# Chunks of the experts' weights: half the rows of one expert in place of a quarter of the rows of two

## The chip, the cores and the metric

The kernel runs on one core of a Trainium2 chip. The metric is the device time of one execution in microseconds (us), the median of three runs. Everything is float32; matrix products run on TensorE (PE in the profile), and 16 DMA engines bring all weights from HBM.

## What is computed

Two transformer blocks on 256 tokens of width 1024. The first has attention and a convolutional feed-forward, the second has attention and a mixture of 32 experts. Only the experts of the second block are touched by the change. Cut to that part, the reference is:

```python
def _hierarchical_moe(h, w_group, w_expert, w_gate, w_up, w_down):
    # top-1 group of 4, then top-2 of its 8 experts; 512 (token, expert) places in all
    ...
    def expert_block(args):
        xb, e = args
        return (jax.nn.silu(xb @ w_gate[e]) * (xb @ w_up[e])) @ w_down[e]
    ...
    contrib = y[dest] * w_sorted[:, None].astype(y.dtype)
    return jnp.zeros((n, d), y.dtype).at[tok_sorted].add(contrib)
```

Each expert has `w_gate` and `w_up` of 1024 x 512 and `w_down` of 512 x 1024, 2 MB each; all 32 experts together have 201 MB, and every one of them is read.

## The kernel before

**Chunks and buffers.** All weights of the program come in chunks of 1 MB (128 partitions x 2048 words), in an order that `plan` writes out. `pump` issues the next chunk's DMA on SP's queue as soon as a buffer is free, `done` counts the uses of a chunk and gives its buffer back, and `give` pumps again. SP's order is thus fixed by the order of the code; a DMA waits for the last reader of its buffer, and for the landing of the DMA eight before it on the same queue (the queue has eight semaphores in rotation).

**Pairs of experts.** The experts are worked off in 16 pairs (pair 0 to pair 15), each expert with up to 64 places. For a pair, expert e = 0 takes columns 0 to 63 of TensorE and expert e = 1 columns 64 to 127: the slice `ps[e * 64:e * 64 + 64, :]` as output puts a product on one half of the array. These products are the rows with `128*64` in the trace, all others take the whole array (`128*128`). `times_x` makes the 16 products of gate or of up (k = 0 to 7, and e = 0, 1 for each k), `down` the 16 of the down matrix (4 rows i, two output halves, two experts).

**A chunk before** (`w_pair`) holds, for both experts of a pair, a quarter of the rows: two runs of 4 KB in each partition. It feeds four products in a row, e = 0, 1, 0, 1, and then its buffer is free. Four chunks make gate, four up, four down; the very last one comes in two pieces.

**What else TensorE does in a pair.** `slots` (rows `bank<-base,hot`, `bank<-wt,hot`) transposes the places of a pair and reads their weights; VectorE (DVE) copies the result out (`ST`, `wslot`, which frees the bank). `gather` (rows `bank<-hot,buf`) collects the tokens of the next two pairs, in four PSUM banks of 8 products each (6 and 2 where the order splits them); it needs `hot`, which VectorE makes in `places`, one instruction for each half of the tokens. `act_T` (rows `bank<-base,act`) transposes the activations, and `combine` (rows `bank<-buf,ST`) adds the former pair's result, 8 products a pair, four for each output half.

**What sets the order.** Only SP's order is the code's own. On all other engines a scheduler orders the instructions at build time, by its own model of when a tile is ready; the engines then run that order as it stands, and wait at semaphores. So the code's `times_x` loop is not one stretch on TensorE: products of `combine`, `slots` and `gather` stand between its products, where the scheduler put them. Where a stretch of `128*64` products ends and a `128*128` product follows, both halves of the array have to be through.

Gate and up of pair 4 and of every even pair after it share their stretch with the first half of a `gather`; those of odd pairs don't.

Of the kernel before, what the change touches and what calls it, by code (L numbers as in the profile page):

```python
# [17 lines left out]
D = 1024  # L18
S = 256
TB = 2  # L20
KT = 8
# [97 lines left out]
class Kernel:  # L119
# [219 lines left out]
    def w_pair(self, src, k, part, pieces=1):  # L339
# [8 lines left out]
                self.nc.sync.dma_start(t[:, :, cs], v[:, :, cs])  # L348
        return load

    def w_tiles(self, src, r0):
        v = src[r0:r0 + 256, :].rearrange("(i p) c -> p i c", p=128)

        def load(t):
            self.nc.sync.dma_start(t.rearrange("p (i c) -> p i c", i=2), v)
        return load
# [52 lines left out]
    def plan(self):  # L409
# [8 lines left out]
        w = a["w_in"][0]  # L418
# [10 lines left out]
        for j in range(16):  # L429
            g = self.fm_units("g", up, j * 256)  # L430
            v = self.fm_units("v", up, 4096 + j * 256)
            if j:
                d += self.row_units("d", dn, j * 256 - 256)
            while len(mods) < min(2 * len(VEC), j // 3 + max(0, j - 1)):
                n, part = VEC[len(mods) // 2], len(mods) % 2
# [9 lines left out]
        w = a["w_in_2"][0]  # L445
# [12 lines left out]
        for pr in range(16):  # L458
            for n, w, k in (("gate", a["w_gate_2"][0], KT), ("up", a["w_up_2"][0], KT), ("down", a["w_down_2"][0], 4)):
                for part in range(4):  # L460
                    load = self.w_pair(w[2 * pr:2 * pr + 2], k, part, 2 if (pr, n, part) == (15, "down", 3) else 1)
                    self.experts[n, pr, part] = self.add_raw(n, load)


    def constants(self):
# [995 lines left out]
    def moe(self):  # L1461
# [12 lines left out]
        xt = self.buf(QK_A, [128, KT, 256])  # L1474
# [22 lines left out]
        where = {pr: (i % 2, j * 128) for i, g in enumerate(groups) for j, pr in enumerate(g)}  # L1497
# [63 lines left out]
        def times_x(pr, n, b):  # L1561
            ps = self.bank(b)
            for k in range(KT):
                c = self.experts[n, pr, k // 2]
                for e in range(2):
                    c0 = e * D + (k % 2) * 512
                    self.mm(ps[e * 64:e * 64 + 64, :], xt[:, k, where[pr][1] + e * 64:where[pr][1] + e * 64 + 64], c.tile[:, c0:c0 + 512],
                            k == 0, k == KT - 1)
                if k % 2:
                    self.done(c)  # L1570
            return ps

# [16 lines left out]
        def down(pr, aT, banks):  # L1589
            ps = [self.bank(b) for b in banks]  # L1590
            for i in range(4):
                c = self.experts["down", pr, i]
                for hf in range(2):
                    for e in range(2):
                        c0 = e * D + hf * 512
                        self.mm(ps[hf][e * 64:e * 64 + 64, :], aT[i // 2][:, i % 2, e * 64:e * 64 + 64],
                                c.tile[:, c0:c0 + 512], i == 0, i == 3)
                self.done(c)
            self.weighted(ps[0], W[pr], gate, 0, y[0])
            return ps[1]  # L1600

# [21 lines left out]
        for what in 'a2 q1 a4 b1 r0 a1 b1 r1 a1 b1 s0 b1 h0 b2 b1 h1 b1 s1'.split():  # L1623
            n = int(what[1])
# [19 lines left out]
        for pr in range(16):  # L1644
            banks, others = ((4, 5), (6, 7))[::1 if pr % 2 == 0 else -1]
            if pr < 15:
                g = times_x(pr, "gate", banks[0])
# [3 lines left out]
            if pr < 15:  # L1651
                u = times_x(pr, "up", banks[1])
# [7 lines left out]
            if pr == 15:  # L1660
                assert self.next_dma == len(self.chunks)
                self.rest_of_experts(xn, A, B, gate, acc, self.free[:3])
                gfin = self.buf(self.free[3], [128, D])
                fin = self.buf(self.free[4], [128, TB, D])
                nc.sync.dma_start(gfin, bass.AP(tensor=a["g_final_2"].tensor, offset=a["g_final_2"].offset,
                                                ap=[[0, 128], [1, D]]))
                g, u = times_x(pr, "gate", banks[0]), times_x(pr, "up", banks[1])
# [83 lines left out]
```

## Time and profile before

| | us |
|---|---|
| median of 3 runs (lowest, highest) | 1072.98 (1071.98, 1074.51) |
| the profiled execution, its own time | 1071.89 |
| its span, first to last instruction | 1070.1 |
| busy: PE | 1011.2 |
| busy: DVE | 511.5 |
| busy: ACT | 406.3 |

The page cuts the span in 40 slices of 26.75 us. The experts' stage begins near 600 us. TensorE is busy in nine tenths or more of almost every slice of the program, and from slice 24 on the DMA engines are too. A matmul of float32 leaves two records in the trace: 16 records of `128*64` products are 8 matmuls, 4 on each half of the array. In a row of the timeline an idle time of the engine stands in brackets, with what ended it.

### The profile page before, as it was taken

Reading aid. Unit: us, or ns where it says so; the run is one execution under the profiler, and the core shown is the slowest. Engines: PE = TensorE matmul, PEld = TensorE weight load, DVE = VectorE, ACT = ScalarE, POOL = GpSimd, SP = SyncE. Lnnn points to the kernel's source line nnn. Section 1 sums busy time; section 2 is a strip of 40 time slices with the busy share of each in tenths; the row PEclk is TensorE's granted clock in tenths of the full one; section 3 lists DMA queues with packets and bytes.
Section 4 is the critical chain, followed back from the end, with each engine's and each line's share of the span. In section 5 each row is a group of like instructions: output and inputs, shape, how many; then the busy total and the mean of one; then the engine's idle time right before and its main releaser. Section 6 shows DMA issues by size and latency. Waiting matters only on the chain. (4 is left out here: it accounts for less than half of the span.)

```text
span 1070.1 us, 14717 instructions
## 1 busy us (share of the span) xinstructions
PE 1011.2 (94%) x5927; PEld 695.7 (65%) x5927; DVE 511.5 (48%) x938; ACT 406.3 (38%) x749; POOL 47.7 (4%) x48
## 2 busy tenths in 40 slices
PE   6999999999999999899999999999999999999986
PEld 6887799999999998699867544443343434333332
DVE  5568588978878866648596311121111111111112
ACT  5566556555455555446664120212020202011112
POOL 2001200000000000200043000000000000000000
PEclk9999999999999999899999799999999999999998
DMA  7964654867576767654555499999999999999994
GB/s 200 374 219 128 235 181 164 309 212 257 203 245 224 268 244 253 200 197 142 192 181 200 169 409 409 409 409 408 409 409 409 409 409 409 409 409 409 409 409 180
DMA packets 131520, 313.52 MB, mean 293 GB/s; under 512 B 7229, under 2 KB 59226, under 8 KB 131450
## 3 DMA queue, kind: packets, MB, share of 16 engines
q1 hardware_dynamic: 131082, 312.02, 78.4%
q0 software_dynamic: 368, 0.54, 0.3%
q8 instruction: 47, 0.77, 0.3%
q14 instruction: 23, 0.19, 0.0%
HBM read 311.89 MB, written 1.05 MB: 292 GB/s over the span
## 5 line engine op out<-in xcount | busy, mean ns | idle before, releaser
L210 PE MATMUL bank<-buf,buf 128*128 128x256 f32 (+4 forms) x4152 | 707.2, 382 | 7.1 <-issue 1.8
L210 PEld LDWEIGHTS bank<-buf,buf 128*128 128x128 f32 (+1 forms) x4152 | 494.8, 177 | 177.1 <-issue 127.0
L185 DVE TENSOR_TENSOR buf<-buf,buf 128x1024 fp32r<-128x1024 f32 x150 | 183.3, 1223 | 72.0 <-ACT buf L183 71.3
L183 ACT ACTIVATE buf<-buf 128x1024 fp32r<-128x1024 f32 x154 | 162.3, 1055 | 111.9 <-PE bank L210 101.4
L210 PE MATMUL bank<-buf,aT 128*64 128x512 f32 x512 | 114.8, 595 | 3.3 <-ACT aT L1586 3.3
L1576 DVE TENSOR_TENSOR act<-act,bank 128x512 f32<-128x512 f32 x16 | 11.0, 687 | 210.2 <-PE bank L210 210.2
L1457 DVE SCALAR_TENSOR_TENSOR tmp<-bank,wslot,gffn 128x512 f32<-128x512 f32 x32 | 24.0, 751 | 133.0 <-PE bank L210 131.3
L210 PEld LDWEIGHTS bank<-buf,aT 128*64 128x64 f32 x512 | 37.1, 137 | 69.3 <-issue 60.2
L1575 ACT ACTIVATE act<-bank 128x512 f32<-128x512 f32 x16 | 9.6, 597 | 137.2 <-PE bank L210 137.2
L1458 ACT ACTIVATE buf<-tmp 128x512 fp32r<-128x512 f32 x32 | 20.2, 631 | 107.5 <-DVE tmp L1457 107.5
L947 ACT ACTIVATE buf<-bank,convT 128x256 f32<-128x256 f32 x64 | 36.0, 563 | 53.7 <-PE bank L210 43.6
L1521 ACT ACTIVATE buf<-bank,mod,g_ffn 128x256 f32<-128x256 f32 (+1 forms) x72 | 34.6, 537 | 48.7 <-PE bank L210 48.7
L1586 ACT ACTIVATE aT<-bank 128x256 f32<-128x256 f32 x32 | 10.6, 382 | 95.1 <-PE bank L213 95.1
L210 PE MATMUL bank<-buf,ST 128*128 128x512 f32 x128 | 38.2, 420 | 8.0 <-ACT buf L1458 7.9
L210 PEld LDWEIGHTS bank<-buf,ST 128*128 128x128 f32 x128 | 21.5, 188 | 36.8 <-ACT buf L1458 18.5
L210 PEld LDWEIGHTS bank<-hot,buf 128*128 128x128 f32 x256 | 32.1, 189 | 17.1 <-issue 8.9
L1030 DVE SCALAR_TENSOR_TENSOR bank<-buf,c,bank 128x512 f32<-128x512 f32 x56 | 42.0, 750 | 1.4 <-DMA buf<-in_w_ada_dram 1.1
L210 PE MATMUL bank<-hot,buf 128*128 128x256 f32 (+1 forms) x256 | 36.7, 290 | 3.6 <-ACT act L1575 3.6
L949 DVE SCALAR_TENSOR_TENSOR buf<-bank,convT,buf 128x255 f32<-128x255 f32 x64 | 30.6, 479 | 10.3 <-ACT buf L947 9.9
L951 DVE SCALAR_TENSOR_TENSOR buf<-bank,convT,buf 128x254 f32<-128x254 f32 x64 | 30.7, 480 | 1.3
L210 PEld LDWEIGHTS bank<-diag,buf 128*128 128x128 f32 x112 | 22.1, 272 | 8.7 <-DVE diag L770 4.6
L210 PE MATMUL bank<-diag,buf 128*128 128x128 f32 x112 | 23.7, 363 | 4.2 <-DVE diag L770 2.7
(202 smaller groups left out, 661.7 us busy)
## 6 DMA issues: line engine op xcount, KB each, us to landing
buf<-in_w_up_dram SPq DMA_DIRECT2D x96, 1024.0 KB, 18.2
buf<-in_w_down_dram SPq DMA_DIRECT2D x79, 1024.0 KB, 18.2
buf<-in_w_gate_dram SPq DMA_DIRECT2D x64, 1024.0 KB, 18.3
buf<-in_w_ada_dram SPq DMA_DIRECT2D x24, 1024.0 KB, 5.2
buf<-in_w_in_dram SPq DMA_DIRECT2D x18, 1024.0 KB, 9.7
buf<-in_w_out_dram SPq DMA_DIRECT2D x8, 1024.0 KB, 17.1
buf<-in_w_in_dram SPq DMA_DIRECT2D x6, 512.0 KB, 7.6
buf<-in_x_dram SPq DMA_DIRECT2D x2, 512.0 KB
```

The costliest lines, as they stand in the source:

```text
L183: pin(nc.scalar.activation(H, raw, AF.Copy))
L185: pin(engine.tensor_tensor(L, raw, H, op=ALU.subtract))
L210: return self.nc.tensor.matmul(out, lhsT, rhs, start=start, stop=stop, skip_group_check=True)
L947: nc.scalar.activation(c[:, s, :], u[:, s, :], AF.Identity, scale=cT[:, 128 + n:129 + n], bias=cT[:, 192 + n:193 + n])
L949: nc.vector.scalar_tensor_tensor(c[:, s, 1:], u[:, s, 0:255], cT[:, 64 + n:65 + n], c[:, s, 1:], op0=ALU.mult, op1=ALU.add)
L951: nc.vector.scalar_tensor_tensor(c[:, s, 2:], u[:, s, 0:254], cT[:, n:n + 1], c[:, s, 2:], op0=ALU.mult, op1=ALU.add)
L1030: nc.vector.scalar_tensor_tensor(p.pa, w, s, p.pa, op0=ALU.mult, op1=ALU.add)
L1457: nc.vector.scalar_tensor_tensor(tmp[:n], ps, w, gate[:n, cs], op0=ALU.mult, op1=ALU.mult)
L1458: nc.scalar.activation(y[:, 0], tmp[:n], AF.Copy)
L1521: nc.scalar.activation(xt[:, k, :n], g, AF.Identity, scale=A[:, k:k + 1], bias=B[:, k:k + 1])
L1576: nc.vector.tensor_tensor(act, act, u, op=ALU.mult)
L1586: nc.scalar.activation(aT[i], pt[:, 2 * i:2 * i + 2, :], AF.Copy)
```

## The change

For all chunks but the down chunks of the last pair, a chunk is now half of the rows of one expert's matrix: one run of 8 KB in each partition (`w_half`). The order of the four chunks of a matrix is: expert 0 first half, expert 1 first half, expert 0 second half, expert 1 second half. Each chunk is still 1 MB, their number and the bytes stay, and each is used by four products of gate or up (k = 0 to 3, or 4 to 7, of one expert), or four of down. In the code `times_x` and `down` name the chunk of each product through the table `self.experts`, and `done` is counted for each product in `times_x`.

```diff
+    def w_half(self, src, k, half):
+        n = src.shape[1] * k // 2
+        v = src.rearrange("(p k) c -> p (k c)", k=k)[:, half * n:half * n + n]
+        def load(t):
+            self.nc.sync.dma_start(t, v)
         return load
...
                 for part in range(4):
-                    load = self.w_pair(w[2 * pr:2 * pr + 2], k, part, 2 if (pr, n, part) == (15, "down", 3) else 1)
-                    self.experts[n, pr, part] = self.add_raw(n, load)
+                    if (pr, n) == (15, "down"):
+                        c = self.add_raw(n, self.w_pair(w[2 * pr:2 * pr + 2], k, part, 2 if part == 3 else 1))
+                        c.left = 2
+                        for e in range(2):
+                            self.experts[n, 2 * pr + e, part] = c, e * D
+                    else:
+                        e, half = part % 2, part // 2
+                        c = self.add_raw(n, self.w_half(w[2 * pr + e], k, half))
+                        c.left = k // 2
+                        for i in range(k // 2):
+                            self.experts[n, 2 * pr + e, k // 2 * half + i] = c, i * 2048 // (k // 2)
...
             for k in range(KT):
-                c = self.experts[n, pr, k // 2]
                 for e in range(2):
-                    c0 = e * D + (k % 2) * 512
-                    self.mm(ps[e * 64:e * 64 + 64, :], xt[:, k, ...], c.tile[:, c0:c0 + 512],
-                            k == 0, k == KT - 1)
-                if k % 2:
+                    c, c0 = self.experts[n, 2 * pr + e, k]
+                    self.mm(ps[e * 64:e * 64 + 64, :], xt[:, k, ...], c.tile[:, c0:c0 + 512], k == 0, k == KT - 1)
                     self.done(c)
...
             for i in range(4):
-                c = self.experts["down", pr, i]
                 for hf in range(2):
                     for e in range(2):
-                        c0 = e * D + hf * 512
+                        c, c0 = self.experts["down", 2 * pr + e, i]
+                        c0 += hf * 512
                         self.mm(ps[hf][e * 64:e * 64 + 64, :], aT[i // 2][:, i % 2, e * 64:e * 64 + 64],
                                 c.tile[:, c0:c0 + 512], i == 0, i == 3)
-                self.done(c)
+                for e in range(2):
+                    self.done(self.experts["down", 2 * pr + e, i][0])
```

In the loop over k the code still names the products in the same order. The scheduler does not keep it. On TensorE, where gate of pair 6 begins (`bank_6544` is gate's bank, `bank_6609` that of `slots`, 5607 to 5610 are `combine`, `bank_6663` the first bank of `gather`), the order before is:

```order
L213 MATMUL bank_6609<-base,hot 128x128 x2
L210 MATMUL bank_6609<-wt,hot 128x2 x2
L210 MATMUL bank_6544<-buf_6314,buf_5567 64x512 x4
L210 MATMUL bank_5607<-buf_5566,ST 128x512
L210 MATMUL bank_5609<-buf_5566,ST 128x512
L210 MATMUL bank_5608<-buf_5566,ST 128x512 x2
L210 MATMUL bank_5610<-buf_5566,ST 128x512 x2
L210 MATMUL bank_6544<-buf_6320,buf_5567 64x512 x4
L210 MATMUL bank_6663<-hot,buf_5560 128x256 x2
```

and after the change:

```order
L213 MATMUL bank_6609<-base,hot 128x128 x2
L210 MATMUL bank_6609<-wt,hot 128x2
L210 MATMUL bank_6544<-buf_6314,buf_5567 64x512
L210 MATMUL bank_5607<-buf_5566,ST 128x512
L210 MATMUL bank_5609<-buf_5566,ST 128x512
L210 MATMUL bank_5608<-buf_5566,ST 128x512 x2
L210 MATMUL bank_5610<-buf_5566,ST 128x512 x2
L210 MATMUL bank_6609<-wt,hot 128x2
L210 MATMUL bank_6663<-hot,buf_5560 128x256 x2
L210 MATMUL bank_6544<-buf_6323,buf_5567 64x512
L210 MATMUL bank_6544<-buf_6314,buf_5567 64x512
```

Before, the four products of one chunk stood together; now the one product of expert 0 (from `buf_6314`) stands alone, its partner of expert 1 (from `buf_6323`) comes after `combine`, the second product of `slots` and two of `gather`.

Further on in TensorE's order, where gate of pair 6 ends and up (`bank_6577`) begins, before:

```order
L210 MATMUL bank_6544<-buf_6406,buf_5567 64x512 x4
L210 MATMUL bank_6630<-hot,buf_5560 128x256 x2
L210 MATMUL bank_6630<-hot,buf_5561 128x256 x2
L210 MATMUL bank_6630<-hot,buf_5560 128x256 x2
L210 MATMUL bank_6577<-buf_6412,buf_5567 64x512 x4
```

and after, from gate's last two products on:

```order
L210 MATMUL bank_6544<-buf_6326,buf_5567 64x512
L210 MATMUL bank_6544<-buf_6410,buf_5567 64x512
L210 MATMUL bank_6577<-buf_6412,buf_5567 64x512
L210 MATMUL bank_6630<-hot,buf_5560 128x256 x2
L210 MATMUL bank_6630<-hot,buf_5561 128x256 x2
L210 MATMUL bank_6630<-hot,buf_5560 128x256 x2
L210 MATMUL bank_6630<-hot,buf_5561 128x256 x2
L210 MATMUL bank_6577<-buf_6422,buf_5567 64x512
```

Here too expert 0's first product of up has moved ahead of the `gather` products, away from its partner (from `buf_6422`).

On VectorE, in the same stretch of pair 6 (two `hot` instructions of `places`, the copies out of `slots`' bank, then the product of the activations), before:

```order
L1459 TENSOR_TENSOR buf_5566<-tmp,buf_5566 128x512
L1527 TENSOR_TENSOR hot<-base,rk 128x256
L1459 TENSOR_TENSOR buf_5566<-tmp,buf_5566 128x512
L1527 TENSOR_TENSOR hot<-base,rk 128x256
L1555 CAST ST<-bank_6609 128x256
L1558 COPY wslot<-bank_6609 64x1 x2
```

and after (line numbers have grown by 18):

```order
L1477 TENSOR_TENSOR buf_5566<-tmp,buf_5566 128x512
L1545 TENSOR_TENSOR hot<-base,rk 128x256
L1477 TENSOR_TENSOR buf_5566<-tmp,buf_5566 128x512
L1573 CAST ST<-bank_6609 128x256
L1576 COPY wslot<-bank_6609 64x1 x2
L1545 TENSOR_TENSOR hot<-base,rk 128x256
```

The second `hot` has moved behind the copies.

## Rows read from the trace of the kernel before

**Rows 1.** The page: the span, and the GB/s of its 40 slices.

```profile
span 1070.1 us, 14717 instructions
GB/s 200 374 219 128 235 181 164 309 212 257 203 245 224 268 244 253 200 197 142 192 181 200 169 409 409 409 409 408 409 409 409 409 409 409 409 409 409 409 409 180
```

**Rows 2.** What the matmuls of PE waited for, 640 to 1034 us (us in total, times, longest).

```profile
PE bank L213 <- DVE act L1576: 9.5, 11, 0.9
PE bank L210 <- ACT buf L1458: 7.2, 11, 0.7
...
PE bank L210 <- PE bank L213: 0.2, 1, 0.2
```

**Rows 3.** Timeline of DVE (start, us): the activations' product of pairs 6 and 8.

```profile
785.35 0.69 DVE L1576 TENSOR_TENSOR act<-act,bank 128x512 f32<-128x512 f32 x1 [15.29 <-PE bank L210]
...
843.95 0.69 DVE L1576 TENSOR_TENSOR act<-act,bank 128x512 f32<-128x512 f32 x1 [15.28 <-PE bank L210]
```

**Rows 4.** DMA, 960 to 1000 us: GB/s in 40 slices, and the packets.

```profile
GB/s 418 406 410 401 422 410 406 406 418 406 410 401 422 406 410 401 414 397 406 414 406 414 406 410 414 410 406 414 406 414 406 414 410 410 410 406 410 414 410 410
DMA packets 4246, 16.37 MB, mean 409 GB/s; under 512 B 252, under 2 KB 252, under 8 KB 4245
```

**Rows 5.** The chunks' tiles, 700 to 1040 us: from a DMA's issue to its landing.

```profile
DMA to landing us min/median/max: 18.2/19.0/21.6
```

**Rows 6.** Timeline of SP and of PE: pair 14's gate, issue and first use.

```profile
974.22 12.03 SPq L348 DMA_DIRECT2D buf<-in_w_gate_dram  x4
...
1000.23 1.94 PE L210 MATMUL bank<-buf,buf 128*64 128x512 f32 x8
```

**Rows 7.** Timeline of PE: gate and up of pair 6.

```profile
765.41 0.51 PE L210 MATMUL bank<-wt,hot 128*128 128x2 f32 x4
765.85 1.94 PE L210 MATMUL bank<-buf,buf 128*64 128x512 f32 x8
767.72 1.65 PE L210 MATMUL bank<-buf,ST 128*128 128x512 f32 x6
769.29 1.94 PE L210 MATMUL bank<-buf,buf 128*64 128x512 f32 x8
...
772.30 3.65 PE L210 MATMUL bank<-buf,buf 128*64 128x512 f32 x16
776.65 0.98 PE L210 MATMUL bank<-hot,buf 128*128 128x256 f32 x6 [0.70 <-ACT act L1575]
...
779.86 5.37 PE L210 MATMUL bank<-buf,buf 128*64 128x512 f32 x24
786.09 0.75 PE L213 MATMUL bank<-base,act 128*128 128x128 f32 x4 [0.86 <-DVE act L1576]
```

**Rows 8.** Timeline of PE: down of pair 1 to gate of pair 3.

```profile
646.02 0.61 PE L210 MATMUL bank<-buf,buf 128*64 128x512 f32 x1 [0.23 <-PE bank L213]
646.27 0.64 PE L210 MATMUL bank<-buf,aT 128*64 128x512 f32 x1
...
653.62 7.18 PE L210 MATMUL bank<-buf,buf 128*64 128x512 f32 x31
...
661.85 7.08 PE L210 MATMUL bank<-buf,buf 128*64 128x512 f32 x30
...
674.88 7.09 PE L210 MATMUL bank<-buf,aT 128*64 128x512 f32 x32
681.80 7.04 PE L210 MATMUL bank<-buf,buf 128*64 128x512 f32 x32
```

**Rows 9.** Timeline of DVE in the stretch of rows 7.

```profile
766.68 0.42 DVE L1527 TENSOR_TENSOR hot<-base,rk 128x256 fp32r<-128x256 f32 x1
769.40 0.42 DVE L1555 CAST ST<-bank 128x256 fp32r<-128x256 f32 x1 [2.31 <-PE bank L210]
769.74 0.32 DVE L1558 COPY wslot<-bank 64x1 f32<-64x1 f32 x2
```

**Rows 10.** Timeline of PE: the first `gather` products after gate in pair 4.

```profile
717.12 0.98 PE L210 MATMUL bank<-hot,buf 128*128 128x256 f32 x6 [0.16 <-ACT act L1575]
```

More of the change, by code (lines that the diff above doesn't have):

```diff
@@ L349, in w_pair @@
         return load
+    def w_half(self, src, k, half):
[3 more added lines that the diff above has]
+            self.nc.sync.dma_start(t, v)
+        return load
     def w_tiles(self, src, r0):
@@ L1563, in times_x @@
             for k in range(KT):
-                c = self.experts[n, pr, k // 2]
                 for e in range(2):
-                    c0 = e * D + (k % 2) * 512
-                    self.mm(ps[e * 64:e * 64 + 64, :], xt[:, k, where[pr][1] + e * 64:where[pr][1] + e * 64 + 64], c.tile[:, c0:c0 + 512],
-                            k == 0, k == KT - 1)
-                if k % 2:
+                    c, c0 = self.experts[n, 2 * pr + e, k]
+                    self.mm(ps[e * 64:e * 64 + 64, :], xt[:, k, where[pr][1] + e * 64:where[pr][1] + e * 64 + 64], c.tile[:, c0:c0 + 512], k == 0, k == KT - 1)
                     self.done(c)
```

## The prediction, made blind

> **What bounds the kernel now.** The change touches only the experts' stage, from about 600 us on. I first read the page's slices: the DMA engines move a flat 409 GB/s in the 16 slices from slice 24 on [rows 1]. A flat line is a full queue, so the first question is whether TensorE waits for the weights. The view of waits says no: among what matmuls waited for between 640 and 1034 us there are DVE, ACT and PE itself, five rows in all, and no DMA [rows 2]. The longest of these waits are the hand-overs within a pair, 0.9 us for the activations' product and 0.7 us for the weighted result. The timeline says the same in another way: the same step of pairs 6 and 8 is 843.95 - 785.35 = 58.6 us apart [rows 3], 29.3 us a pair. The queue needs more than that: a pair is 12 chunks of 1.0486 MB, 12.58 MB / 409 GB/s = 30.8 us [rows 4]. Both can hold only because the stage starts with a stock of landed chunks that TensorE eats up. How much of it is left near the end: pair 14's gate chunks are issued from 974.22 us on and first used at 1000.23 us [rows 6]; a chunk lands at most 21.6 us after its issue [rows 5], so at 995.8 us, and 4.4 us are left. TensorE's order of work sets the end, DMA is 4 us behind it, and anything that lengthens TensorE's stage counts in full.
>
> **The change part by part: the transfers.** The 188 chunks in the new shape have the same bytes and the same place in SP's queue; SP issues as many instructions. The packets now are nearly all 4 KB or less (16.37 MB / 4246 = 3.9 KB, [rows 4]); no row shows an 8 KB run. Bounds for its speed: from no gain to the best short slices, 422 GB/s against 409 [rows 4]. Either way it is worth nothing while TensorE is behind the stock; I take nothing. The Trainium skill's page "DMA: Bandwidth & Descriptors" (section on why small descriptors are slow) puts a fixed 3 cycles on each packet of 32-byte beats; by it, as an estimate, 128 + 3 beats twice against 256 + 3 once is 1.1% less time, and its ceiling of 435 GB/s would leave 425 GB/s for 4 KB runs, where the rows have 409. If DMA set the end, the sum by that rule would be about 5 us lower.
>
> **The chunk's two users.** Expert 1's first half is needed right behind expert 0's, not one chunk (four products, 1.8 us) later, and expert 0's buffer comes back some four products later. Price: 1.8 us of the 4.4 us that are left at pair 14, none of it on the path; behind a late chunk TensorE would wait with everything queued on it. If TensorE gets slower, the stock grows and this is covered further.
>
> **TensorE's order.** This is the part that costs. The unit: 24 records of half-array products last 5.37 us, 16 last 3.65 us [rows 7]; 8 records are 4 products, two on each half, so one product takes (5.37 - 3.65) / 2 = 0.86 us and two of different experts run side by side in it. A stretch between two full-array products therefore lasts as many units as its fuller half has products. The trace has one case with a half product set apart. Up of pair 2 had its first expert-0 product pulled ahead of `combine`. The rest, 30 records, lasts 7.08 us, no less than 32 records with 7.04 us [rows 8]: the missing product saves nothing. And the stretch that had it in front lasts 653.62 + 7.18 - 646.02 = 14.78 us against 681.80 + 7.04 - 674.88 = 13.96 us for one without [rows 8]: 0.82 us more. So a product set apart from its partner costs one unit of 0.82 to 0.86 us.
>
> Now the two orders, stretch by stretch. Before, gate and up of a pair are cut at whole chunks (4, 4, 8, 4 and 12 products in pair 6), 16 units in every pair. After, pair 6 has 1, 7, 1, 8 and 15 products, which is 1 + 4 + 1 + 4 + 8 = 18 units. Pairs 4, 8, 10 and 12 are cut alike, and pair 14 into 1, 16, 7, 1 and 7, 18 units too. Pairs 5, 7, 9, 11 and 13 have 1 and 31 products, 17 units. That is 6 x 2 + 5 x 1 = 17 units more, 17 x 0.86 = 14.6 us. Pairs 0 to 3 and 15 keep their stretches; the number of stretches and thus of changes between half and full array stays the same in all.
>
> **A new wait.** In pairs 6, 8, 10 and 12 two `gather` products now follow `combine` and the second `slots` product directly. Their bank is that of `slots`, which DVE frees, and their second operand is the `hot` that moved behind these copies. In the rows DVE begins the cast 769.40 - 769.29 = 0.11 us after `combine` ends, ends the two copies at 769.74 + 0.32 = 770.06, and `hot` takes 0.42 us more [rows 9]: ready 1.2 us after `combine`. TensorE has one `slots` product to do meanwhile, half of 765.85 - 765.41 = 0.44 us [rows 7]. So it waits 1.0 us, with all products of gate queued behind; before, four products (769.29, [rows 7]) covered this. Four such waits are 4.0 us. In pairs 4 and 14 one or sixteen products stand in between and cover it, and in odd pairs nothing asks for the bank. Bounds: none of it (if copies and cast run earlier than I read) to 1.2 us each, 0 to 4.8 us.
>
> The wait for ACT between gate and the first `gather` products of gate's bank, 0.70 us [rows 7], stays: up's first product moved into it runs beside the last of gate, not behind it. In pair 4 it was 0.16 us [rows 10], since other `gather` products stood there; I add 0.5 us. The wait of 0.86 us ahead of the transposes [rows 7] and that for the weighted result stay.
>
> In `down` the order of experts turns from 0, 1, 0, 1 to 0, 0, 1, 1 at one or two places in pairs 4 to 13. I take it as free: at 646.27 us an expert-1 product of down starts 0.25 us after the set-apart expert-0 product, although another expert-0 product stands between the two in the order and cannot have started [rows 8]. Expert 1's half does not wait for expert 0's. If it did, it would cost one unit in each of ten pairs, 8.6 us.
>
> **The sum.** 14.6 + 4.0 + 0.5 = 19.1 us on the path; against the profiled execution's own 1071.89 us that is 1091.0 us. The median of the runs lies 1.1 us above that execution, so I forecast 1092 us, 1.8% slower. Own range: units at 0.82 us and no new wait give 1072.98 + 13.9 = 1087 us; waits of 1.2 us and 0.1 us for each second `slots` product apart give 1072.98 + 20.9 = 1094 us.
>
> **The rivals.** First, faster: the queue sets the end after all, and longer runs speed it up. For it: the queue is full over 16 slices of 26.75 us, 428 us [rows 1]. Against: no matmul waits for it [rows 2], and 4.4 us are in hand. At 422 GB/s the 428 us would shrink by 428 x 13 / 422 = 13.2 us, to 1060 us. It decides only if TensorE's own stage does not grow.
>
> Second, no change: a product set apart is free, because the half it leaves empty is filled by what comes next, and DVE has freed the bank early. Then 1073 us. Against: the 0.82 us measured in rows 8. With the four waits alone it would be 1077 us.
>
> Third, slower by more: the 0, 0, 1, 1 order in `down` costs a unit in each of ten pairs. For it: within one half the order is kept. Against: 646.27 us in rows 8. 1092 + 8.6 = 1101 us.
>
> Fourth, the hand-over: buffers that come back later and chunks needed earlier empty the stock, and the pair takes the queue's 30.8 us instead of 29.3 us in the last third, five pairs, less the 4.4 us in hand: 5 x 1.5 - 4.4 = 3 us, 1076 us. Against: a TensorE that needs about 31.2 us a pair never catches up with the queue.
>
> **How the numbers follow.** Forecast 0.74 (1087 to 1094), third rival 0.10 (up to 1101), no change 0.06, waits alone or hand-over 0.05, faster 0.05. A measurement of this kernel tells apart about 0.2%, or 2.1 us: faster 0.05, same 0.06, slower 0.89. For 8 in 10 the range has to reach from the forecast's lower end, with some room for a unit or a wait that is hidden, to the third rival: 1085 to 1101 us.
>
> **What would show it.** Right: the same step of pairs 6 and 8 some 62.2 us apart (58.6 + 3 x 0.86 + 1.0); single records of half products ahead of `combine`, with the next row a unit later; a bracket of about 1.0 us with DVE as releaser at two `gather` products in pairs 6, 8, 10 and 12; SP waiting for PE, and GB/s in the stage at about 12.58 MB / 31.1 us = 404 instead of a flat 409; down still 7.1 us for 32 records. Wrong: matmuls that wait for a DMA, the step still 58.6 us apart although the order moved, or down at 7.9 us.

## The result: 1.4% slower, and the profile after

| | before | after |
|---|---|---|
| median of the runs on one chip, us | 1072.80 (4 runs, 1071.98 to 1074.51) | 1087.82 (4 runs, 1085.99 to 1088.87) |
| the profiled execution, its own time | 1071.89 | 1088.87 |
| its span | 1070.1 | 1087.1 |

The ratio is 1.0136, with a 95% interval of 1.0117 to 1.0155: 15.0 us by the medians. The two profiled executions are 17.0 us apart.

The page after, span and GB/s of the 40 slices (27.2 us each), beside [rows 1]:

```profile
span 1087.1 us, 14713 instructions
GB/s 202 377 233 133 194 175 214 251 235 268 235 230 217 287 186 262 198 189 130 263 153 119 289 419 420 420 420 419 420 420 419 420 420 421 419 420 420 419 160 39
```

The queue is as full as before, at 420 GB/s in place of 409, and it is through earlier: slice 39 begins at 1032.7 us and is filled for 160 / 420 of it, so the weights are in at about 1043 us by this estimate; the trace has the last chunk's landing at 1044.2 us. Before, slice 40 began at 1043.3 us and was filled for 180 / 409: about 1055 us (the last landing is at 1055.1 us). TensorE ends 17 us later, the queue 11 us earlier.

DMA after, 960 to 1000 us, beside [rows 4]:

```profile
DMA packets 2304, 16.80 MB, mean 420 GB/s; under 512 B 255, under 2 KB 255, under 8 KB 255
```

and the chunks' tiles, 700 to 1040 us, from a DMA's issue to its landing, beside [rows 5]:

```profile
DMA to landing us min/median/max: 8.5/16.0/21.3
```

Nearly all packets are 8 KB now. A chunk lands after 8.5 us at best, where it was 18.2 us, though the rate rose by 2.7% only. That fits fewer transfers standing in the queue: more of the buffers hold chunks that have landed.

What the matmuls waited for after the change, 640 to 1034 us (us in total, times, longest), beside [rows 2]:

```profile
PE bank L213 <- DVE act L1591: 8.5, 10, 0.9
PE bank L210 <- ACT buf L1476: 6.5, 10, 0.7
PE bank L210 <- ACT act L1590: 4.1, 6, 0.7
PE bank L210 <- DVE wslot L1576: 3.4, 4, 0.8
```

The two rows left out are ACT's `aT`, 2.8 us, and PE itself, 0.2 us. Still no DMA. One line is new: four waits for DVE's copy `wslot`, 3.4 us.

DVE after, the activations' product of pairs 6, 7 and 8 (start, us), beside [rows 3]:

```profile
791.63 0.69 DVE L1591 TENSOR_TENSOR act<-act,bank 128x512 f32<-128x512 f32 x1 [18.43 <-PE bank L210]
820.56 0.69 DVE L1591 TENSOR_TENSOR act<-act,bank 128x512 f32<-128x512 f32 x1 [13.29 <-PE bank L210]
853.68 0.69 DVE L1591 TENSOR_TENSOR act<-act,bank 128x512 f32<-128x512 f32 x1 [18.44 <-PE bank L210]
```

Pairs 6 and 8 are 853.68 - 791.63 = 62.05 us apart, against 58.6 us in [rows 3].

TensorE after, gate and up of pair 6, beside [rows 7] (start, duration, instruction, number of records; in brackets the idle time and what ended it):

```profile
769.26 1.07 PE L210 MATMUL bank<-buf,buf 128*64 128x512 f32 x2
770.27 1.66 PE L210 MATMUL bank<-buf,ST 128*128 128x512 f32 x6
771.76 0.28 PE L210 MATMUL bank<-wt,hot 128*128 128x2 f32 x2
772.88 0.47 PE L210 MATMUL bank<-hot,buf 128*128 128x256 f32 x2 [0.84 <-DVE wslot L1576]
773.28 3.65 PE L210 MATMUL bank<-buf,buf 128*64 128x512 f32 x14
776.86 0.74 PE L210 MATMUL bank<-hot,buf 128*128 128x256 f32 x4
777.53 1.07 PE L210 MATMUL bank<-buf,buf 128*64 128x512 f32 x2
778.53 0.50 PE L210 MATMUL bank<-hot,buf 128*128 128x256 f32 x2
778.96 3.65 PE L210 MATMUL bank<-buf,buf 128*64 128x512 f32 x16
783.30 1.21 PE L210 MATMUL bank<-hot,buf 128*128 128x256 f32 x8 [0.68 <-ACT act L1590]
784.44 7.08 PE L210 MATMUL bank<-buf,buf 128*64 128x512 f32 x30
```

In pair 5 (an odd pair; no `gather` among its products):

```profile
741.76 1.07 PE L210 MATMUL bank<-buf,buf 128*64 128x512 f32 x2
742.76 1.66 PE L210 MATMUL bank<-buf,ST 128*128 128x512 f32 x6
744.26 0.28 PE L210 MATMUL bank<-wt,hot 128*128 128x2 f32 x2
744.47 13.95 PE L210 MATMUL bank<-buf,buf 128*64 128x512 f32 x62
```

In pair 6 two stretches hold one product (2 records) each, and each takes 1.00 us until the next row starts. Pair 5 has one such stretch. The 14 records at 773.28 us take 3.65 us, as long as the 16 at 778.96 us: the partner that has gone ahead leaves its place empty.

The step from one pair's activations' product to the next pair's (differences of starts in the same DVE timeline; the rows of pairs 7 and 8 after the change stand above) splits the loss. Start to end of the first four pairs (0 to 3) differs by less than 0.1 us.

| pair | before | after | difference |
|---|---|---|---|
| 4 | 29.67 | 31.66 | +1.99 |
| 5, 7, 9, 11, 13 | 28.16 to 28.17 | 28.92 to 28.93 | +0.76 each, 3.8 |
| 6, 8, 10, 12 | 30.43 to 30.44 | 33.11 to 33.12 | +2.68 each, 10.7 |
| 14 | 30.17 | 31.78 | +1.61 |
| 15 | 30.77 | 28.78 | -1.99 |
| from there to the end | 19.86 | 19.86 | 0 |

The sum is +16.1 us. The other 0.9 us between the two spans lies ahead of pair 0's product (614.4 and 615.3 us), in code that the change doesn't touch; over the profiled executions of this text that point lies between 612.6 and 616.1 us.

Pair 15 is the only pair that got faster. TensorE there before the change:

```profile
1034.19 3.65 PE L210 MATMUL bank<-buf,buf 128*64 128x512 f32 x16 [0.56 <-PEq L1356]
1039.62 10.52 PE L210 MATMUL bank<-buf,buf 128*64 128x512 f32 x48 [1.77 <-issue]
1050.07 0.44 PE L213 MATMUL bank<-base,hot 128*128 128x128 f32 x2
```

and after:

```profile
1053.18 13.95 PE L210 MATMUL bank<-buf,buf 128*64 128x512 f32 x64 [0.57 <-PEq L1374]
1067.06 0.44 PE L213 MATMUL bank<-base,hot 128*128 128x128 f32 x2
```

Ahead of pair 15's products each engine takes a branch (`rest_of_experts`). Before, TensorE did eight products behind it, stood still for 1.77 us, with nothing that it waited for in the profile ("issue"), and went on. After, 64 records run through. Before, the queue was full at this time; after, the last chunk had landed 8 us ahead of TensorE's branch.

### The profile page after: what moved, and what is told of

Read it like the earlier page. It is cut to its first block, busy times and chain, and to the rows that moved or that the text cites. A ratio compares the mean times of both kernels' runs of the same rounds, so it can differ in the third digit from the quotient of the medians.

```text
span 1087.1 us, 14713 instructions
## 1 busy us (share of the span) xinstructions
PE 1026.1 (94%) x5927; PEld 705.8 (65%) x5927; DVE 512.3 (47%) x938; ACT 406.8 (37%) x749; POOL 48.0 (4%) x48
## 3 DMA queue, kind: packets, MB, share of 16 engines
HBM read 311.89 MB, written 1.05 MB: 288 GB/s over the span
## 5 line engine op out<-in xcount | busy, mean ns | idle before, releaser
L210 PE MATMUL bank<-buf,buf 128*128 128x256 f32 (+4 forms) x4152 | 720.7, 381 | 7.8 <-DVE buf L284 2.6
L210 PEld LDWEIGHTS bank<-buf,aT 128*64 128x64 f32 x512 | 40.7, 137 | 66.2 <-issue 58.2
## 6 DMA issues: line engine op xcount, KB each, us to landing
buf<-in_w_gate_dram SPq DMA_DIRECT2D x64, 1024.0 KB, 16.1
```

Of the source, the lines that this page charges most:

```text
L210: return self.nc.tensor.matmul(out, lhsT, rhs, start=start, stop=stop, skip_group_check=True)
```

## The experiments

In all of them TensorE's units are counted as in the prediction: 495 in the program before the change, 512 after. Steps are those of the table above. Each ratio is against the kernel before the change, run on the same chip.

### Does the order cost the time, or the chunk?

The changed kernel with its chunks, but expert 1's product named ahead of expert 0's. Expert 1's chunk lands second, so that no product is ready without its partner, and the scheduler leaves the two together: 495 units.

```diff
             for k in range(KT):
-                for e in range(2):
+                for e in (1, 0):
                     c, c0 = self.experts[n, 2 * pr + e, k]
```

> The changed kernel, all new chunks and their order of transfer kept, but gate and up name expert 1's product ahead of expert 0's for each row k. In the order that results no product stands apart from its partner: gate and up are again 16 units a pair (495 units in the whole program, as before the change; the changed kernel has 512), and there are 20 stretches of half-array products fewer (57 in place of 77). Two `gather` products still follow `combine` directly, but the second `hot` stands ahead of the copies again. Theory of the order (the loss is TensorE's units and the waits they bring): all of it comes back; against 1072.8 us before the change some 20 changes between half and full array go too, about 0.1 us each, so 1069 to 1073 us. Theory of the chunks (the loss is in the new chunks themselves: what they hold, when they are needed and released, the order of experts in `down`): it stays at 1085 to 1088 us. Apart from that: pair 15's 1.8 us of standing still behind the branch, gone after the change, should be back here if it hangs on weights that still come in while TensorE takes the branch (1.8 us within the 1069 to 1073), and stay away if it hangs on the new chunks.

1073.19 us, ratio 1.0012 (0.9995 to 1.0029). The loss is gone but for a rest, with every new chunk in place: it was the order, not what the chunks hold. By the steps 2.2 us of the 16.1 us stay, less than the 4.2 us of the waits named next: pair 4 takes 31.58 us, 1.9 us more than before the change, pairs 6, 8, 10 and 12 take 0.25 to 0.37 us more, odd pairs 0.16 us less. The 2 us that 20 changes between half and full array fewer were to give back don't show in the sum. One expectation failed: five `gather` products wait 0.84 us for `wslot` although the second `hot` stands ahead of the copies. TensorE and DVE in that kernel, pair 6:

```profile
767.75 1.77 PE L210 MATMUL bank<-buf,ST 128*128 128x512 f32 x6
769.56 0.42 DVE L1573 CAST ST<-bank 128x256 fp32r<-128x256 f32 x1 [0.49 <-PE bank L210]
769.90 0.32 DVE L1576 COPY wslot<-bank 64x1 f32<-64x1 f32 x2
770.37 1.17 PE L210 MATMUL bank<-hot,buf 128*128 128x256 f32 x8 [0.84 <-DVE wslot L1576]
```

The cast starts when `combine` ends, 1.7 us after the last `slots` product. And pair 15's standing still is back; in the view of waits, 640 to 1050 us:

```profile
PE bank L210 <- issue: 1.6, 1, 1.6
```

### The half changes

Gate and up in the old chunks, `down` in the new:

```diff
+                    elif n != "down":
+                        c = self.add_raw(n, self.w_pair(w[2 * pr:2 * pr + 2], k, part))
+                        c.left = 4
+                        for e in range(2):
+                            for i in range(2):
+                                self.experts[n, 2 * pr + e, 2 * part + i] = c, e * D + i * 512
                     else:
                         e, half = part % 2, part // 2
```

> Gate and up as before the change (a quarter of the rows of both experts), only `down` in the new chunks. TensorE's order has 16 units a pair as before (495); `down` has the order 0, 0, 1, 1 at two places in each of pairs 4 to 13; the second product of `slots` stands behind `combine`, with four products ahead of the next `gather`. Prediction's theory (0, 0, 1, 1 is free, and four products cover the copies): 1071 to 1074 us, `down` 7.1 us for 32 records. Third rival (each pair loses a unit of 0.86 us in `down`): 8.6 us more, 1081 us, `down` 7.9 us.

1071.37 us, ratio 0.9999 (0.9983 to 1.0015). Two of its `down` rows (pairs 4 and 5):

```profile
730.45 7.26 PE L210 MATMUL bank<-buf,aT 128*64 128x512 f32 x32
757.24 7.14 PE L210 MATMUL bank<-buf,aT 128*64 128x512 f32 x32 [0.47 <-ACT aT L1607]
```

With 0, 0, 1, 1 at two places, 32 records take 7.14 to 7.27 us against 7.09 us before, not 7.9 us. Expert 1's half doesn't wait for expert 0's.

Gate and up in the new chunks, `down` in the old:

```diff
-                    if (pr, n) == (15, "down"):
-                        c = self.add_raw(n, self.w_pair(w[2 * pr:2 * pr + 2], k, part, 2 if part == 3 else 1))
+                    if n == "down":
+                        c = self.add_raw(n, self.w_pair(w[2 * pr:2 * pr + 2], k, part, 2 if (pr, part) == (15, 3) else 1))
```

> `down` as before the change, only gate and up in the new chunks. TensorE has the same 512 units as the changed kernel, with the same products set apart; but `slots` is whole again ahead of `combine`, and on DVE the second `hot` stands ahead of the copies, so that the copies run beside `combine` and the `gather` products behind it find their bank free. Theory of the order, units and wait apart: the four waits of 0.84 us go, 3.4 us of the changed kernel's 1087.8, so 1084 to 1085 us, and no `gather` product waits for DVE. If the waits were only a place where time shows that is lost elsewhere, it stays at 1087 to 1088 us.

1088.08 us, ratio 1.0152 (1.0107 to 1.0198). The whole loss is in gate and up. The expectation failed all the same: the four waits of 0.84 us stay, although `slots` is whole and `hot` out of the way. TensorE and DVE, pair 6:

```profile
768.95 1.65 PE L210 MATMUL bank<-buf,ST 128*128 128x512 f32 x6
770.63 0.42 DVE L1573 CAST ST<-bank 128x256 fp32r<-128x256 f32 x1 [1.44 <-PE bank L210]
770.97 0.32 DVE L1576 COPY wslot<-bank 64x1 f32<-64x1 f32 x2
771.43 0.47 PE L210 MATMUL bank<-hot,buf 128*128 128x256 f32 x2 [0.84 <-DVE wslot L1576]
```

Again the cast waits until `combine` ends. My reason for the wait fell here: it isn't the second `slots` product or `hot`. What cast and `combine` share is `ST`, a single buffer that `combine` reads and the cast overwrites. [rows 9] has the same cast 0.11 us behind `combine`, with 2.31 us of idle time in front of it; only, before, four products stood between `combine` and the `gather` that needed the bank.

Up and `down` in the new chunks, gate in the old (in the diff of the first half change `n == "gate"` in place of `n != "down"`): only up's first product stands apart, in six pairs.

> Gate as before the change, up and `down` in the new chunks. Now only up's first product of expert 0 stands apart, in each even pair from 4 to 14: 501 units, six more than before the change, and no `gather` directly behind `combine`. Theory of the units: 6 x 0.85 = 5.1 us over the kernel before the change, 1076.5 to 1078 us, all of it in the even pairs and nothing in the odd ones; pair 15's 1.7 us behind the branch stay (weights still come in). If a product apart costs less in this place, since it runs beside the last product of gate, a pair's step shows it: below 0.5 us in an even pair, 1072 to 1075 us.

1076.09 us, ratio 1.0048 (1.0031 to 1.0066). Pairs 6, 8, 10 and 12 take 31.19 to 31.22 us, +0.75 to 0.79; pair 4 +0.80, pair 14 +0.83; odd pairs -0.05. Six units cost 4.7 us, 0.79 us each, beside the last product of gate as elsewhere.

### The buffer of `ST`

The kernel with expert 1 named first, and `ST` in two buffers by turns:

```diff
-            st = self.t([128, TB, 128], "ST", F32R, tag="dist")
+            st = self.t([128, TB, 128], "ST", F32R, tag=("dist", "convT")[pr % 2])
```

> The kernel with expert 1 named first (1073.2 us), with one more edit: the copy `ST` of `slots` alternates between two buffers in place of one. TensorE's order is the same, instruction by instruction. In that kernel's trace `gather` waits 0.84 us for DVE in five pairs, and each time DVE's cast begins 0.1 us behind the last product of `combine`. Theory of the one buffer (the cast overwrites the `ST` that `combine` reads, and so can't begin before `combine` is through): the five waits go, 4.2 us, 1069.0 us, below the kernel before the change (1071.7 to 1072.8). Theory of the bank (the cast is late because DVE or `slots` is late): the waits stay, 1073 us. Pair 15's 1.6 us behind the branch stay in either case.

1071.01 us, ratio 0.9989 (0.9979 to 0.9998). TensorE and DVE, pair 6:

```profile
767.34 1.77 PE L210 MATMUL bank<-buf,ST 128*128 128x512 f32 x6
768.24 0.41 DVE L1573 CAST ST<-bank 128x256 fp32r<-128x256 f32 x1
769.04 1.18 PE L210 MATMUL bank<-hot,buf 128*128 128x256 f32 x8
```

The cast runs beside `combine`, and `gather` waits no more: the one buffer is shown as the cause. In time it gave less than the 4.2 us of the five waits. The even pairs from 4 to 12 became 0.8 to 1.0 us faster, four of the five odd pairs (5, 7, 9 and 13) 0.33 to 0.35 us slower, and pair 14 0.33 us slower. The traces show where: with its buffer free early, the cast now stands ahead of the second half of the weighted result on DVE, which the later products of `combine` read. In pair 5 that result (`buf<-tmp,buf`) starts 1.67 us behind `combine`'s first product in place of 0.90 us, right behind the cast, and the last six records of `combine` take 1.98 us in place of 1.65 us. The same 1.97 to 2.00 us stand in pairs 7, 9, 13 and 14; in pair 11, where the cast did not move ahead of that result, they still take 1.65 us, and its step did not grow.

The same waits, taken away in the changed kernel by work in front of them:

```diff
+                    if (n, k, e) == ("gate", 3, 1):
+                        self.cover = i
...
+                            if i == 3 and len(group) == 2:
+                                self.tc.add_manual_dep(m.ins, self.cover.ins.name, mybir.DependencyInfo(
+                                    mybir.DependencyClass.NoSync, mybir.DependencyReason.DATA))
```

> The changed kernel with one order pinned: the `gather` products whose bank is that of `slots` stand behind gate's products of row 3, in place of directly behind `combine` (in pairs 6, 8, 10 and 12). 512 units as in the changed kernel, the same products stand apart, and so do the stretches; only the four waits have work in front of them again. Theory that the four waits are on the path: 3.4 us less than the changed kernel's 1087.8, 1084 to 1085 us, and no wait for DVE's `wslot`. Rival: the time is lost again at the next wait (the copies of `modulate`, the silu), 1087 to 1088 us.

1084.45 us, ratio 1.0114 (1.0098 to 1.0129). No `wslot` line among the waits; pairs 6, 8, 10 and 12 take 32.04 to 32.06 us, 1.06 us less. The waits were on the path, and nothing took their place.

### The runs of 8 KB

The changed kernel, all orders unchanged, with chunks of two runs of 4 KB of one expert:

```diff
-        v = src.rearrange("(p k) c -> p (k c)", k=k)[:, half * n:half * n + n]
+        v = src.rearrange("(p k) c -> p (k c)", k=k).rearrange("p (a b n) -> p a b n", a=2, b=2)[:, :, half, :]
...
-                            self.experts[n, 2 * pr + e, k // 2 * half + i] = c, i * 2048 // (k // 2)
+                            row = i // (k // 4) * (k // 2) + half * (k // 4) + i % (k // 4)
+                            self.experts[n, 2 * pr + e, row] = c, i * 2048 // (k // 2)
...
-            for k in range(KT):
+            for k in (0, 1, 4, 5, 2, 3, 6, 7):
...
-            for i in range(4):
+            for i in (0, 1, 2, 3) if pr == 15 else (0, 2, 1, 3):
```

> The changed kernel with the same order on TensorE, DVE and ACT, instruction by instruction, but each chunk made of two runs of 4 KB in each partition (rows 0, 1, 4, 5 and 2, 3, 6, 7 of each eight of one expert) in place of one run of 8 KB. Theory of the order: the size of the runs doesn't set the end, 1087 to 1090 us; the stage's GB/s goes back from 420 to 409 if the run's size made the difference, and stays at 420 if what the chunk holds made it. If pair 15's standing still of 1.8 us hangs on weights still coming in: the last ones land near 1055 us at 409 GB/s, the branch is taken near 1053 us, so part of it or all may come back (0 to 1.8 us). If longer runs had given back time anywhere else on the path, it is slower than 1090 us.

1087.15 us, ratio 1.0154 (1.0115 to 1.0192). Its page has

```profile
GB/s 203 377 235 133 195 175 213 253 233 270 231 237 209 296 196 244 229 167 145 249 155 117 287 409 409 409 409 409 409 409 408 410 409 409 409 409 409 409 339 39
```

So the length of the runs makes the 420 GB/s, not what a chunk holds; and with TensorE this slow it is worth nothing. Pair 15's standing still did not come back: its 64 records run through, and its step is 28.89 us against 28.78 us, although the last 0.7 MB of weights were still coming in when TensorE took its branch at 1049.70 us. The next section takes this up.

### The branch of pair 15

The changed kernel with seven loads more behind the last chunk, so that the queue is busy at the branch:

```diff
                 assert self.next_dma == len(self.chunks)
+                for i in range(7):
+                    self.w_half(a["w_gate_2"][0][i], KT, 0)(self.buf(self.free[5 + i % (len(self.free) - 5)], [128, 2048]))
```

> The changed kernel with seven more 1 MB loads queued behind its last chunk, into free buffers, read by nobody; TensorE's, DVE's and ACT's order stays, instruction by instruction. In the changed kernel the weights have landed by 1044 us, TensorE takes its branch near 1052.4 us, the first 16 KB instruction load after it starts 1.0 us later, and TensorE doesn't stand still between pair 15's products. Before the change the queue is full at the branch, that load starts 3.7 us behind it, and TensorE stands still for 1.77 us. With the spare loads the queue is busy until about 1061 us. Theory of the code load (it queues behind the weights): the load starts some 3.5 us behind the branch again, TensorE stands still for 1.6 to 1.8 us, and pair 15's step grows from 28.8 to 30.6 to 30.8 us; 1089 to 1090 us. Rival (the standing still hangs on something else that the change moved, such as the order ahead of the branch or on SP): 28.8 us, 1087 to 1088 us.

1090.40 us, ratio 1.0172 (1.0142 to 1.0202). TensorE behind the branch:

```profile
1054.07 4.05 PE L210 MATMUL bank<-buf,buf 128*64 128x512 f32 x17 [0.55 <-PEq L1374]
1058.68 10.52 PE L210 MATMUL bank<-buf,buf 128*64 128x512 f32 x47 [0.57 <-issue]
1069.13 0.44 PE L213 MATMUL bank<-base,hot 128*128 128x128 f32 x2
```

It stands still again behind the first eight products, and the first 16 KB load of instructions starts 2.9 us behind TensorE's branch (1056.21 - 1053.29), against 1.0 us in the changed kernel (1053.42 - 1052.40) and 3.7 us before (1037.08 - 1033.42). But it is 0.57 us, not 1.6 to 1.8, and the step grows by 1.17 us (28.78 to 29.95), not 2; the step shows the effect, since part of the 2.6 us between the two medians lies outside pair 15. The rate was not lower: from the branch to the load the spare loads moved 426 GB/s, the weights before the change 405. What was less is the amount still to come: at the branch 1.2 MB of the loads issued had not yet moved, against 6.2 MB before the change.

The other kernels on record agree. Here is what was still to come at TensorE's branch (loads issued less packets moved), how far behind the branch the first load of instructions started, and how long TensorE stood still:

| kernels | still to come, MB | load starts, us behind the branch | TensorE stands still, us |
|---|---|---|---|
| changed; only gate and up new; `gather` behind gate | 0 | 1.0 to 1.1 | 0 |
| changed, with 4 KB runs | 0.7 | 1.6 | 0 |
| changed, with spare loads | 1.2, and 1.0 more issued 1.3 us later | 2.9 | 0.57 |
| before, and the other eight of this text | 2.3 to 6.4 | 3.6 to 3.7 | 1.36 to 1.84 |

Where TensorE stands still, it goes on 2.5 to 2.8 us after that load's start; its first eight products take about 3.7 us, so that a load that starts early enough is hidden behind them. That the load of instructions waits behind the weights, and TensorE for the load, fits all fourteen traces, and the spare loads show its direction by an experiment. Pair 15's step fell by 2.0 us, 1.77 us of it standing still; the remaining 0.2 us is not explained.

### Is there a faster kernel, and is 8 KB worth something in it?

The longest wait left is TensorE's for DVE's product of the activations, 0.9 us in 11 pairs. `slots` takes 0.65 us and can stand there. Expert 1 named first, one `ST`, and `slots` pinned behind up (`self.last` is up's last product):

```diff
             for tb in range(TB):
-                self.tr(pt[:, tb * 128:(tb + 1) * 128], s[:, tb], self.ident)
+                i = self.tr(pt[:, tb * 128:(tb + 1) * 128], s[:, tb], self.ident)
+                if pr < 15:
+                    self.tc.add_manual_dep(i.ins, self.last.ins.name, mybir.DependencyInfo(
+                        mybir.DependencyClass.NoSync, mybir.DependencyReason.DATA))
```

> The kernel with expert 1 named first (1073.2 us; one buffer for `ST`), and `slots` pinned behind up in each pair from 4 on, so that its products stand in front of the transposes that wait 0.85 to 0.89 us for DVE's product, and the bank of `slots` is no longer in the way of a `gather` behind `combine`. TensorE's units stay 495. Theory that TensorE's order and its waits set the end: `slots` takes 0.65 us, which now lies in that wait, in 11 pairs 7 us; the five waits for `wslot` go, 4.2 us; 1061 to 1064 us. The queue at 420 GB/s should just keep up: the last chunk had 16.3 us in hand in that kernel, so some 5 us are left. Rival: the queue comes into the path (30.0 us a pair against TensorE's 28.3) and matmuls wait for a DMA in the last pairs: 1064 to 1068 us.

1064.41 us, ratio 0.9936 (0.9920 to 0.9952): the fastest here, 0.6% ahead of the kernel before the change. It is 0.4 us above the range expected, and not by the rival, which wanted waits for a DMA: an even and an odd pair together became 1.9 us faster (pairs 6 and 7: 56.9 us against 58.8), where 2.1 us were expected. TensorE at the end of up of pair 6:

```profile
781.63 0.44 PE L213 MATMUL bank<-base,hot 128*128 128x128 f32 x2
781.90 0.51 PE L210 MATMUL bank<-wt,hot 128*128 128x2 f32 x4
782.58 0.75 PE L213 MATMUL bank<-base,act 128*128 128x128 f32 x4 [0.18 <-DVE act L1594]
```

The wait of 0.86 us ahead of the transposes [rows 7] is 0.18 us. No matmul waits for a DMA, and none for `wslot`.

The same order with runs of 4 KB (the edit of the section on 8 KB on top):

> The same order on TensorE and DVE, instruction by instruction, with chunks of two runs of 4 KB in each partition. With TensorE this fast the queue at 409 GB/s has to come into the path: in the kernel with two buffers for `ST` and 4 KB runs the last chunk had 0.7 us in hand at 1071.8 us, and this order wants its weights 8 us earlier. Theory of the queue: matmuls wait for a DMA in pairs 13 to 15, and the time is 1070 to 1072 us, 8 us behind the kernel with 8 KB runs. Rival (the size of the runs doesn't matter at any speed of TensorE): within 2 us of that kernel.

1072.08 us, ratio 1.0001 (0.9986 to 1.0016). Its view of waits (640 to 1034 us) has a DMA:

```profile
PE bank L210 <- DMA buf<-in_w_up_dram: 4.2, 4, 1.5
```

and its timeline of TensorE shows one of the places, in up of pair 13:

```profile
984.02 3.65 PE L210 MATMUL bank<-buf,buf 128*64 128x512 f32 x16 [1.47 <-DMA buf<-in_w_up_dram]
```

Pairs 11 to 14 take 30.59 to 30.71 us each, the 30.8 us of 12.58 MB at 409 GB/s. Here the queue sets the time, and 8 KB runs are worth 7.7 us.

The kernel with two buffers for `ST`, with 4 KB runs, lies between:

> The same with expert 1 named first and two buffers for `ST`, but with chunks of two runs of 4 KB in each partition; TensorE's order as in the kernel with 8 KB. If TensorE alone sets the end: the same time as with 8 KB, 1069 us. If the queue, at 409 GB/s in place of 420, now comes into the path: a pair takes it 30.8 us, before the change 4.4 us were in hand at pair 14's gate and 2.4 us at the last chunk, TensorE is 3 to 4 us earlier here and wants both experts' chunks at once: matmuls wait 1 to 3 us for a DMA in pairs 13 to 15, and the time is 1070 to 1073 us.

1071.79 us, ratio 1.0001 (0.9990 to 1.0013), against 1071.01 us with 8 KB. Up to pair 14 the queue keeps up. In pair 15 it doesn't quite: the view of waits (640 to 1050 us) names no DMA, but has

```profile
PE bank L210 <- SPq L1375: 0.6, 1, 0.6
```

ahead of the last eight products of up. SP, behind its own branch, takes the landings of the chunks one after the other; by the order of its semaphores the one that it had just taken, at 1045.28 us, is that of up's last chunk. Pair 15 takes 31.54 us in place of 30.79 us, and that is the whole difference between the two kernels (0.80 us from pair 3's product to the end). The price expected, 1 to 3 us from pair 13 on, was too high.

The kernel before the change, with `slots` pinned behind up and nothing else:

> The kernel before the change, old chunks (two runs of 4 KB, both experts), with nothing but `slots` pinned behind up. TensorE would be 7 us faster by the wait that `slots` now fills. The last chunk had 2.4 us in hand at 1072.8 us, and the queue moves 409 GB/s. Theory of the queue: no more than 2 to 3 us come of it, 1069 to 1072 us, and matmuls wait for a DMA near the end. Rival (the queue has more in hand than the landings say): 1065 to 1067 us.

1067.50 us, ratio 0.9962 (0.9949 to 0.9975), between the two ranges: more than the queue was expected to leave, less than the rival. Matmuls wait 1.7 us for DMAs, and from pair 13 on a pair takes 30.4 to 31.1 us. It is queue-bound at the end too, but it got there two pairs later than the kernel with 4 KB runs of one expert. Which part of those 4.6 us is the chunk's shape (both experts' chunks wanted at once) and which the other order was not separated.

## Why the prediction was right, and where it was off

Forecast 1092.0 us (1085 to 1101), slower; measured 1087.82 us. Step by step:

**The bound.** Right: TensorE's order sets the end, no matmul waits for a DMA after either.

**The transfers.** Worth nothing, as taken; the kernel with 4 KB runs and the same order takes as long. The rate of 420 GB/s is close to the upper bound of 422. A view was foretold wrong: not 404 GB/s and a queue held back by TensorE, but a flat 420. The buffers' stock had shrunk to 4.4 us before; a slower TensorE and a faster queue let it grow through the whole stage (a pair takes TensorE some 31 us and the queue 12.58 MB / 420 GB/s = 30.0 us), and the stage ended before it was full. The Trainium skill's page "DMA: Bandwidth & Descriptors" (section "Why small descriptors are slow (HBM only)") gives, as the estimate in the prediction worked out from it, 1.1% for 8 KB against 4 KB. The rows have 420 / 409, 2.7%, so here the measurement decides.

**The units.** 17 x 0.86 = 14.6 us foretold. Measured: odd pairs 5 x 0.76; pairs 6, 8, 10 and 12 2.68 - 0.84 = 1.84 each for two; pair 4 1.99 - 0.52 = 1.47; pair 14 1.61; in all 14.2 us. The third rival, a unit in `down`, fell with the half change of `down`; "no change" fell with the rows of pair 6, where 14 records last as long as 16.

**The new wait.** At the four places named, with the releaser named, 0.84 us in place of 1.0: 3.4 us against 4.0. The cause was half right: DVE frees the bank late, but because its cast has to wait for `combine`, the reader of the only `ST`; the `hot` that moved does not matter, since TensorE started at 772.88 us, while that `hot` ran from 772.76 to 773.19. The prediction used the 0.11 us between `combine` and the cast in [rows 9] as a length and didn't ask why the cast stood there with 2.31 us of idle time in front. That the size came out near is luck in part: 0.42 us of the 1.0 us were that `hot`; without it the prediction's own rows give 770.06 - 769.29 - 0.22 = 0.55 us.

**Pair 4's silu.** 0.68 us against 0.16 us, +0.52; foretold 0.5.

**The hand-over and faster.** None of either.

**The step that failed: pair 15.** The prediction let it keep its time, since its stretches stay. They do, but it held 1.77 us of standing still behind a branch, from 1037.8 us on, just past the 1034 us at which the prediction's view of waits ended [rows 2]. With the queue empty at the branch that went away, and the step fell by 2.0 us. So the path grew by 14.2 + 3.4 + 0.5 - 2.0 = 16.1 us in place of 19.1.

From 1092.0 to 1087.8 us, then: 2.0 us pair 15; 1.0 us units and waits; less 0.9 us that the profiled execution lost ahead of the experts; and 2.1 us because the median before lies 1.1 us above its profiled execution and the median after 1.05 us below. The last two are the scatter of single executions.

The step of pairs 6 and 8, foretold as 62.2 us, was 62.05.

## What to carry to other kernels

When two products share the array, ask which transfer makes each of them ready: if a chunk feeds only one of the two, a scheduler that goes by readiness splits the pair, and naming the later one first held it together here, with the order of one loop changed (1087.8 to 1073.2 us). Read what a copy waits for before taking its wait as given; an idle time of 2.31 us ahead of a small cast was a single buffer, and it was harmless only as long as other work happened to stand behind it. A faster transfer shows in the time only once the engine that hid it is faster: the same 8 KB runs were worth nothing at 1087 us and 7.7 us at 1064 us.

## What the runs showed of the hardware that was not expected

- Runs of 8 KB in a partition moved 419 to 421 GB/s over 15 slices in a row, runs of 4 KB 408 to 410 GB/s with the same order on all engines (the slices that the transfers fill).
- Behind TensorE's branch the first 16 KB load of instructions started 3.6 to 3.7 us late with 2.3 MB or more of weights still to come (nine kernels), 2.9 us with 1.2 MB, 1.6 us with 0.7 MB and 1.0 to 1.1 us with none (three kernels); TensorE stood still for 1.36 to 1.84, 0.57, 0 and 0 us behind the first eight products.
- Within `down`, 0, 0, 1, 1 in place of 0, 1, 0, 1 cost 0.05 to 0.18 us in 7.1 us; a product set apart by whole-array work cost 0.74 to 0.92 us.
- Fewer changes between half and whole array gave little: with 57 stretches of half-array products in place of 77 (expert 1 first, two buffers for `ST`) the time from pair 3's product to the end was 372.2 us against 373.0 us.
